# A hybrid decoder step on one core: the attention's heads run together, and two more pairs of convolution blocks move to a seven-product scheme

## The chip, the cores and the metric

The kernel runs on one core of a Trainium2 chip. The core has a matrix engine (TensorE, PE in the profile, with its weight loads shown as PEld), a vector engine (VectorE, DVE), an engine for functions of one operand (ScalarE, ACT), a general one (GpSimd, POOL) and one that mainly issues transfers (SyncE, SP). Each engine works through its own instructions in order; they wait for one another through semaphores. The metric is the time of one launch in microseconds of device time, the median of several runs. Lower is better.

## The reference, cut to what matters

One layer of a decoder for 512 new tokens of a prompt and 8 single tokens of running sequences, 520 rows of width 2048. All is float32.

```python
def mixer(xn, conv_prev, gla_prev, w_in, conv_w, gate_w2, gate_b, gla_norm_g, w_out, chunk):
    proj = xn @ w_in
    bg, cg, hin, q, k, v, og, glr = jnp.split(proj, [_S1, _S2, _S3, _S4, _S5, _S6, _S7], axis=-1)
    cu, conv_new = causal_dwconv(cg * hin, conv_prev, conv_w)
    ya = bg * cu
    logf = jax.nn.log_sigmoid((glr @ gate_w2 + gate_b).astype(f32)) / GATE_TAU
...
    o, s_new = gla_chunked(qh, kh, vh, lf, gla_prev.astype(f32), chunk)
    o = o * lax.rsqrt(var + EPS) * gla_norm_g.astype(f32).reshape(GLA_HEADS, GLA_DV)
    yb = (o.reshape(Bn, L, GLA_V_DIM) * jax.nn.silu(og.astype(f32))).astype(xn.dtype)
    out = jnp.concatenate([ya, yb], axis=-1) @ w_out
```

`w_in` has 6160 columns: three blocks of 1024 for the convolution mixer (bg from column 0, cg from 1024, hin from 2048), q and k (512 each, from 3072 and 3584: 128 for each of four heads), v (1024 from 4096), og (1024 from 5120) and 16 for the gate. After the mixer come a residual sum, a norm, an up projection to 2 x 5632 columns with a convolution and a gate, a down projection, a second residual and a last norm.

## The kernel before

Activations lie transposed, 128 channels to a partition block, 520 tokens along the row, cut into two halves of 260. A float32 product is made of three matmuls of reduced precision: every operand is split into a high part (`hi`, ScalarE) and a rest (`lo`, VectorE), and hi x hi, lo x hi and hi x lo are added up in the matrix engine's banks.

**Classical groups.** `group()` (line 213) makes 128 output columns from all 2048 inputs: 16 steps `k`, each of 3 matmuls for 2 token halves, 96 matmuls of 128 x 128 by 260. Its weights come as two halves of 512 KB. `fetch()` asks SP for the next half named in the list `ahead`, `high()` and `low()` split it, `next_half()` takes one that is split. At the steps `k` in `BEATS` (3, 7, 11, 15) the group calls `beat()` (line 157): one entry of `soon`, one step of the first generator in `queue`, one entry of `side`. At its end it takes one step of the generator in `extra`.

**The attention.** `gla_head()` (line 934) is a generator for one head and needs 22 calls. Steps 1 to 3 make the decay, step 4 the first scores. In steps 7 to 13 it runs through seven levels: in each, matmuls of the products `L` give scores (line 1051 for the first level, 1066 for the others), VectorE merges them into `at` (1073), VectorE makes the `L` that is due two steps later (991) from `e`, and POOL and ScalarE prepare an `e` for a later step (285, 984). Sample states `s0` are loaded with `vb`, their values, read back from memory (1015, 1019), scaled on ScalarE (1025) and updated on VectorE (1028). Step 14 transposes `kc`, steps 15 to 18 treat four chunks of 128 tokens with a running sum `S` (1134, 1139, 1148, 1150, 1152), and steps 19 to 22 normalise the output and store it to `o_d` (1195).

**Order of the first part.** For each head `h` the loop at line 1233 runs groups for k, q and the two halves of v (the first head's k and q come from the start of the kernel), puts `gla_head(h)` in the queue and then runs `conv_tile(h - 1)`; after the loop comes `conv_tile(3)`. `conv_tile(j)` (line 865) is three groups (cg, hin, bg) with the convolution put in `side`, and for an odd `j` the sums and splits that the output projection needs (`mixed_done`). That is 26 groups. From head 1 on `extra` holds `mixer_sums()` (line 774), which reads the normalised input back in four parts and makes the sums that the mixer pairs need; it takes 21 calls. The scratch of the attention (pool `gla`) is given up at the end of this part, and the tiles that come next use the same memory.

**Mixer pairs.** Then two more groups (og of the first head) run while the first pair is prepared. A pair (line 812, `MIX`) makes two blocks of 128 columns at once as a 2 x 2 block product with seven products instead of eight: 7 x 8 x 3 = 168 matmuls by 260. ("ch", j) makes the cg and hin blocks of convolution tile j, ("b", j) the bg blocks of tiles j and j+1, ("og", j) two og blocks. Each product needs its own split weights, prepared two products ahead (`prepare`, lines 1370 and 1374); the seven weight operands are sums of four loaded tiles, made on VectorE (1315), one of them by an accumulating transfer on POOL's queue (1319) for every pair but the first. Generators in `steps` (`mix_gate`, `leave`) finish a pair beside the next one and store its forms to `g_d`. The same scheme then serves the output, up and down projections.

The order of instructions on every engine, POOL and SP included, is the order of the program in both parts (`InOrder`).

Of the kernel before, what the change touches and what calls it, by code (L numbers as in the profile page):

```python
# [17 lines left out]
P = 128  # L18
# [6 lines left out]
NH = 4  # L25
DV = 256
# [11 lines left out]
def trunk_kernel(  # L38
# [53 lines left out]
    def tmp():  # L92
        return tp.tile([P, T], F32, tag="t", name="t")
# [37 lines left out]
    def halves(t):  # L131
        return t[:, :HT], t[:, HT:T]
# [11 lines left out]
    soon, queue, side, extra = deque(), deque(), deque(), deque()  # L144
# [12 lines left out]
    def beat():  # L157

        if soon:
            soon.popleft()()  # L160
        if queue:
            try:
                next(queue[0])
            except StopIteration:
                queue.popleft()
        if side:
            side.popleft()()
# [5 lines left out]
    def new_mm():  # L173

        return [mmp.tile([P, 512], F32, tag="mm", name="mm") for _ in range(2)]

    def span(ps, w, acts, k0, pk0, nk, nkt):

        outs = [x[:, :HT] for x in ps]
        for k in range(k0, k0 + nk):  # L180
            mm3(outs, (w[0][:, k - pk0, :], w[1][:, k - pk0, :]), acts[k], k == 0, k == nkt - 1)

    ahead, coming, highs, halved = deque(), deque(), deque(), deque()
# [13 lines left out]
    def low():  # L197
        if highs:
            raw, nk, hi = highs.popleft()
            lo = wp.tile([P, 1024], F32R, tag="lo", name="lo")  # L200
            nc.vector.tensor_tensor(lo, raw, hi.bitcast(F32), op=ALU.subtract)
            halved.append([x.rearrange("p (k c) -> p k c", k=nk) for x in (hi, lo)])
            fetch()

    def next_half():

        w = halved.popleft()
        high()
        return w

    BEATS = (3, 7, 11, 15)

    def group():
        ps = new_mm()
        for k in range(KD):
            if k % 8 == 0:
                w = next_half()
            span(ps, w, xa, k, k // 8 * 8, 1, KD)
            if k in BEATS:
                beat()  # L220
            if k % 8 == 3:
                low()
        if extra and next(extra[0], extra) is extra:
            extra.popleft()
        return ps


# [98 lines left out]
    with ExitStack() as es:  # L326
# [3 lines left out]
        def tps():  # L330
            return tpp.tile([P, 1024], F32, tag="tp", name="tp")
# [43 lines left out]
        cols = (3584, 3072)  # L375
# [44 lines left out]
        ps = tps()  # L420
# [175 lines left out]
    def evac(ps, out, r=R):  # L596
        for o, p, rr in zip(halves(out), ps, halves(r)):
            nc.vector.tensor_tensor(o, p[:, :HT], rr, op=ALU.mult)
# [18 lines left out]
    def conv(z, w, taps, j, st):  # L617


        c = tmp()  # L620
        conv_tap(c, z, w, taps, j)
        conv_rest(c, z, w, taps, j, st)
        return c
# [34 lines left out]
    def next_z():  # L658
        zcount[0] += 1
        return zpad[zcount[0] % 2]  # L660
# [113 lines left out]
    def mixer_sums():  # L774
# [35 lines left out]


    MIX = (
        ("ch", 4), ("og", 2), ("ch", 5), ("og", 4), ("b", 4), ("og", 6), ("ch", 6), ("ch", 7),
        ("b", 6),
    )

    def mix_source(n, m, k):
# [23 lines left out]
    with ExitStack() as mix:  # L841
# [23 lines left out]
        def conv_tile(j):  # L865
            ps = group()
            cgr = tmp()
            evac(ps, cgr[:, :T])
            ps = group()
            hr = tmp()  # L870
            evac(ps, hr[:, :T])
            z = next_z()
            nc.vector.tensor_tensor(z[:, 2:], cgr[:, :T], hr[:, :T], op=ALU.mult)
            keep_last(z, j, 8, new_conv_p, new_conv_s)
            c = []
            side.append(lambda: c.append(conv(z, cw, 8, j, stc[:, j, :])))
            ps = group()
            bgr, ya = tmp(), tmp()[:, :T]
            if j % 2 == 0:
                even[j] = ya = z[:, 2:]  # L880
            evac(ps, bgr[:, :T])
            nc.vector.tensor_tensor(ya, bgr[:, :T], c[0][:, :T], op=ALU.mult)
            mixed_done(j, ya)

        in_order = InOrder(nc.gpsimd.engine, nc.sync.engine).after_all()
        with ExitStack() as gl:
# [12 lines left out]
                    base=-32 * j, pattern=[[-1, NS]], channel_multiplier=1,  # L899
                )  # L900
            w2s = gp.tile([96, 512], F32R, name="w2s")
            for h in range(NH):
                tile_cols = (3584 + h * P, 3072 + h * P, 4096 + h * DV, 4096 + h * DV + P)
                for c0 in (*tile_cols, *(x + (h - 1) * P for x in (1024, 2048, 0)))[
                    slice(3, 4) if h == 0 else slice(None)
                ]:
                    ahead += [(0, c0), (8, c0)]
            ahead += [(k0, c0) for c0 in (1408, 2432, 384, 5120, 5248) for k0 in (0, 8)]
            halved += v0
            for _ in range(3):  # L910
                fetch()
# [300 lines left out]
            def first_scaled(k, q):  # L1212
                nc.vector.tensor_tensor(k, kq[0], R, op=ALU.mult)
                nc.vector.scalar_tensor_tensor(
                    q, kq[1], QSCALE, R, op0=ALU.mult, op1=ALU.mult
                )
# [16 lines left out]
            for h in range(NH):  # L1233
                if h == 1:
                    extra.append(mixer_sums())
                ps = group() if h else None
                k = gp.tile([P, T], F32, tag="qk", name="k", bufs=5)
                if h:
                    evac(ps, k)
                ps = group() if h else None  # L1240
                assert done[0] >= h - 1
                q = gp.tile([P, T], F32, tag="qk", name="q", bufs=5)
                if h:
                    for o, p, rr in zip(halves(q), ps, halves(R)):
                        nc.vector.scalar_tensor_tensor(
                            o, p[:, :HT], QSCALE, rr, op0=ALU.mult, op1=ALU.mult
                        )
                else:
                    soon += [
                        lambda: None, factors_out, lambda: first_scaled(k, q), first_gate,  # L1250
                        gate_weights,
                    ]
                vt = gp.tile([P, 4, DV], F32, tag="vt", name="vt", bufs=2)
                v = []
                for d in range(2):
                    ps = group()
                    t = gp.tile([P, T], F32, tag="v", name="v", bufs=2)
                    evac(ps, t)
                    v.append(t)
                    soon.append(lambda: None)  # L1260
                    soon.append(lambda t=t, vt=vt, d=d: v_rows(t, vt, d, 0, 4))
                soon.append(lambda v=v, h=h: v_samples(v, h))
                queue.append(gla_head(h, q, k, vt))
                if h:
                    conv_tile(h - 1)
            conv_tile(NH - 1)
            for _ in range(3):
                side.popleft()()
            assert not queue and not extra and not soon, (len(queue), len(extra), len(soon))
# [527 lines left out]
    ps = new_mm()  # L1797
# [19 lines left out]
    ps = new_mm()  # L1817
# [37 lines left out]
    for i, (kind, at, r) in enumerate(order):  # L1855
        j, n = i % 7, i // 7
# [41 lines left out]
        if i in (0, 2, NW, NW + 2):  # L1898

            x = xq[1, 0][0]  # L1900
# [204 lines left out]
```

## Time and profile before

| | us |
|---|---|
| median of 3 runs | 2143.29 |
| lowest and highest | 2142.72, 2144.54 |
| the profiled execution, its own time | 2143.29 |
| its span, first to last instruction | 2141.5 |
| mean granted TensorE clock | 0.998 of full |

The page gives, for one execution, the busy time of each engine, a picture of the span in 40 slices of 53.5 us, the transfer queues, the chain of work that ended last followed back from the end, and the costliest groups of instructions. A row of the timeline or of the chain begins with the start in us and the length in us; a row of a group ends with busy time, mean length of one instruction in ns, and the idle time of the engine ahead of it. L991 is line 991 of the kernel before. The spans of the parts that matter here: the classical groups from about 52 us to 437.5 us, nine mixer pairs to about 622 us, the output projection to about 785 us, the up projection after it.

### The profile page before, as it was taken

The page shows a single profiled execution, that of the slowest core. Times are in us where ns is not written, and L with a number is a line of the kernel's source. Part 1 is how long each engine was busy: PE and PEld are TensorE (multiplying, and loading weights), DVE is VectorE, ACT ScalarE, POOL GpSimd, SP SyncE. Part 2 cuts the span into 40 slices and gives each one's busy share as a digit, 9 for nine tenths or more (in the row PEclk, how much of TensorE's full clock was granted, in tenths as well). Part 3 has the DMA queues.
Part 4 walks back from the last instruction along what each step waited for, and adds up shares of the span by engine and source line. Part 5 has one row for each costly group of instructions (what it writes and reads, how often), then busy time and mean ns, then how long its engine had stood idle before and what let it go on. Part 6 is the DMA issues. An engine that isn't in the chain of part 4 may idle for free.

```text
span 2141.5 us, 44283 instructions
## 1 busy us (share of the span) xinstructions
PE 2117.8 (99%) x17952; PEld 2097.2 (98%) x17952; DVE 1747.0 (82%) x2333; ACT 1105.2 (52%) x1662; POOL 434.9 (20%) x622
## 2 busy tenths in 40 slices
PE   9999999999999989999999999999999999999997
PEld 8999999999999989999999999999999999999997
DVE  6457576688979898998998988988989778888886
ACT  7434434355544686555555555555555554444445
POOL 4213223111334311111211221212212300200000
PEclk9999999999999999999999999999999999999999
DMA  8445473597898996676676676676676966994734
GB/s 257 129 134 176 132 206 114 147 253 187 223 287 239 267 287 164 173 190 177 179 185 174 181 184 174 180 187 175 178 188 180 298 203 163 276 291 133 225 109 159
DMA packets 467325, 415.74 MB, mean 194 GB/s; under 512 B 21721, under 2 KB 426473, under 8 KB 466977
## 3 DMA queue, kind: packets, MB, share of 16 engines
q1 hardware_dynamic: 424209, 289.84, 47.7%
q0 software_dynamic: 42864, 123.00, 21.9%
q8 instruction: 141, 2.31, 0.4%
q14 instruction: 63, 0.52, 0.1%
q10 hardware_dynamic: 48, 0.07, 0.0%
HBM read 299.65 MB, written 80.31 MB: 177 GB/s over the span
## 4 chain that ended last, share of the span: by engine, by line
PE 87%; DMA 5%; DVE 4%; issue 2%; POOL 1%; ACT 1%; SPq 1%; ACTq 0%; DVEq 0%; POOLq 0%
PE mm L1394 34%; PE mm L140 15%; PE ms L1394 14%; PE x L1637 7%; PE y L1637 7%; PE f L1637 3%; PE e L1637 3%; DVE lo L1374 1%; DMA x_d<-acc 1%; DMA form<-g_d 1%; DMA raw<-in_w_in_dram 1%; DMA wgraw<-in_w_in_dram 1%; DVE acc L1656 1%; PE ms L1066 1%; DMA g_d<-fh 0%
## 5 line engine op out<-in xcount | busy, mean ns | idle before, releaser
L1394 PE MATMUL mm<-yl,hi 128*128 128x260 f32 x1696 | 477.2, 281 | 3.5 <-DVE yl L124 3.5
L1394 PE MATMUL mm<-yh,hi 128*128 128x260 f32 x1696 | 475.9, 281 | 1.3 <-ACT ms L1404 0.7
L1394 PE MATMUL mm<-yh,lo 128*128 128x260 f32 x1696 | 475.3, 280 | 1.4 <-DVE lo L1374 1.4
L1370 ACT ACTIVATE hi<-raw 128x1024 fp32r<-128x1024 f32 x324 | 341.8, 1055 | 242.2 <-issue 90.1
L1374 DVE TENSOR_TENSOR lo<-raw,hi 128x1024 fp32r<-128x1024 f32 x324 | 396.1, 1222 | 44.3 <-ACT hi L1370 40.8
L1374 DVE TENSOR_TENSOR lo<-s,hi 128x1024 fp32r<-128x1024 f32 x243 | 298.5, 1228 | 124.4 <-ACT hi L1370 124.2
L1370 ACT ACTIVATE hi<-s 128x1024 fp32r<-128x1024 f32 x243 | 256.7, 1056 | 220.6 <-PE ms L1394 93.6
L1394 PEld LDWEIGHTS mm<-yl,hi 128*128 128x128 f32 x1696 | 318.9, 188 | 4.1 <-DVE yl L124 4.1
L1394 PEld LDWEIGHTS mm<-yh,lo 128*128 128x128 f32 x1696 | 319.9, 189 | 1.8 <-DVE lo L1374 1.8
L1394 PEld LDWEIGHTS mm<-yh,hi 128*128 128x128 f32 x1696 | 319.8, 189 | 1.7 <-ACT ms L1404 0.9
L1394 PE MATMUL ms<-b,hi 128*128 128x260 f32 x1408 | 265.7, 281 | 0.0
L1394 PEld LDWEIGHTS ms<-b,hi 128*128 128x128 f32 x1408 | 222.8, 189 | 0.0
L1637 PE MATMUL x<-form,hi 128*128 128x260 f32 x1120 | 211.8, 281 | 0.9 <-ACT f L1662 0.5
L1637 PE MATMUL y<-form,hi 128*128 128x260 f32 x1120 | 211.5, 281 | 0.0
L1315 DVE TENSOR_TENSOR s<-s,raw 128x1024 f32<-128x1024 f32 x162 | 198.0, 1222 | 2.8
L1394 PE MATMUL ms<-b,lo 128*128 128x260 f32 x704 | 197.4, 280 | 0.0
L1637 PEld LDWEIGHTS x<-form,hi 128*128 128x128 f32 x1120 | 176.5, 188 | 1.7 <-issue 0.8
L1637 PEld LDWEIGHTS y<-form,hi 128*128 128x128 f32 x1120 | 176.5, 188 | 0.3
L1637 PE MATMUL x<-form,lo 128*128 128x260 f32 x560 | 157.0, 280 | 0.4 <-DVE lo L1374 0.4
L1637 PE MATMUL y<-form,lo 128*128 128x260 f32 x560 | 156.8, 280 | 0.0
L1394 PEld LDWEIGHTS ms<-b,lo 128*128 128x128 f32 x704 | 132.4, 188 | 0.0
L1394 PE MATMUL mm<-bh,hi 128*128 128x260 f32 x424 | 118.8, 280 | 1.0 <-DVE acc L1656 1.0
(402 smaller groups left out, 5005.1 us busy)
## 6 DMA issues: line engine op xcount, KB each, us to landing
raw<-in_w_up_dram SPq DMA_DIRECT2D x176, 512.0 KB, 5.1
raw<-in_w_down_dram SPq DMA_DIRECT2D x96, 512.0 KB, 5.6
raw<-in_w_in_dram SPq DMA_DIRECT2D x92, 512.0 KB, 4.3
form<-f_d SPq DMA_DIRECT2D x126, 260.0 KB, 6.1
raw<-raw POOLq DMA_DIRECT2D x56, 512.0 KB, 5.9
f_d<-t POOLq DMA_DIRECT2D x80, 260.0 KB, 5.5
raw<-in_w_out_dram SPq DMA_DIRECT2D x32, 512.0 KB, 9.3
form<-g_d POOLq DMA_DIRECT2D x42, 260.0 KB, 7.6
```

Of the source, the lines that this page charges most:

```text
L140: nc.tensor.matmul(o, w, xx, start=first and i == 0, stop=last and i == 2)
L1066: nc.tensor.matmul(pb[t, c * 32 : (c + 1) * 32], L[:, c, t], second(L[:, c : c + 1, t])[:, 0], start=True, stop=True, tile_position=(0, t. ...
L1315: return lambda: nc.vector.tensor_tensor(out, x, y, op=ALU.add)
L1370: nc.scalar.activation(his[i], src, AF.Copy)
L1374: nc.vector.tensor_tensor(los[i], src, his[i].bitcast(F32), op=ALU.subtract)
L1394: nc.tensor.matmul(st["bank"][b], w[:, k, :], x, start=b not in st["used"] and k == 0 and j == 0, stop=k == 7 and j == 2, skip_group_check ...
L1637: nc.tensor.matmul(ps[:, m, :], w[:, k, m * P : (m + 1) * P], x, start=b not in st["used"] and k == 0 and j == 0, stop=k == 3 and j == 2, ...
L1656: nc.vector.tensor_tensor(a, a, inner(bk[b]), op=op)
```

## The change

Convolution tiles 2 and 3 leave the classical part and become three mixer pairs, ("ch", 2), ("ch", 3) and ("b", 2), among the first in `MIX`, which now has 12 entries. The heads' groups run one after another, k, q, v, v of each, and `conv_tile(0)` and `conv_tile(1)` follow after all of them. The first part has 20 groups. `BEATS` has five entries for a group in place of four. In the k and q groups of heads 1 to 3, `group(True)` takes a step of `extra` after `k` = 7 as well as at the end. The list of weight halves follows the new order.

```diff
-    BEATS = (3, 7, 11, 15)
-
-    def group():
+    BEATS = (2, 5, 8, 11, 14)
+
+    def further():
+        if extra and next(extra[0], extra) is extra:
+            extra.popleft()
+
+    def group(twice=False):
...
-        if extra and next(extra[0], extra) is extra:
-            extra.popleft()
+            if k == 7 and twice:
+                further()
+        further()
         return ps
...
     MIX = (
-        ("ch", 4), ("og", 2), ("ch", 5), ("og", 4), ("b", 4), ("og", 6), ("ch", 6), ("ch", 7),
-        ("b", 6),
+        ("ch", 2), ("og", 2), ("ch", 3), ("og", 4), ("b", 2), ("ch", 4), ("og", 6), ("ch", 5),
+        ("b", 4), ("ch", 6), ("ch", 7), ("b", 6),
     )
...
-            for h in range(NH):
-                tile_cols = (3584 + h * P, 3072 + h * P, 4096 + h * DV, 4096 + h * DV + P)
-                for c0 in (*tile_cols, *(x + (h - 1) * P for x in (1024, 2048, 0)))[
-                    slice(3, 4) if h == 0 else slice(None)
-                ]:
-                    ahead += [(0, c0), (8, c0)]
-            ahead += [(k0, c0) for c0 in (1408, 2432, 384, 5120, 5248) for k0 in (0, 8)]
+            cols = [4096 + P]
+            for h in range(1, NH):
+                cols += [3584 + h * P, 3072 + h * P, 4096 + h * DV, 4096 + h * DV + P]
+            for j in range(2):
+                cols += [1024 + j * P, 2048 + j * P, j * P]
+            ahead += [(k0, c0) for c0 in (*cols, 5120, 5248) for k0 in (0, 8)]
...
-                ps = group() if h else None
+                ps = group(True) if h else None
                 k = gp.tile([P, T], F32, tag="qk", name="k", bufs=5)
                 if h:
                     evac(ps, k)
-                ps = group() if h else None
+                ps = group(True) if h else None
...
                 queue.append(gla_head(h, q, k, vt))
-                if h:
-                    conv_tile(h - 1)
-            conv_tile(NH - 1)
+            for j in range(2):
+                conv_tile(j)
```

## The prediction

> **What bounds the kernel now.** I read the page from the top: the busy times, the slices, the chain that ended last, then TensorE's waits.
>
> ```profile
> span 2141.5 us, 44283 instructions
> ...
> PE 2117.8 (99%) x17952; PEld 2097.2 (98%) x17952; DVE 1747.0 (82%) x2333; ACT 1105.2 (52%) x1662; POOL 434.9 (20%) x622
> ...
> PEclk9999999999999999999999999999999999999999
> ...
> PE 87%; DMA 5%; DVE 4%; issue 2%; POOL 1%; ACT 1%; SPq 1%; ACTq 0%; DVEq 0%; POOLq 0%
> ```
>
> ```profile
> PE mm L1394 <- DVE yl L124: 3.5, 3, 1.9
> PE mm L1394 <- DVE lo L1374: 1.4, 2, 1.0
> ...
> PE ms L1134 <- DVE at L1073: 0.2, 1, 0.2
> ```
>
> TensorE (PE) is busy 99% at full clock, the chain is 87% TensorE, and its longest waits are a few microseconds in all. So time goes down only with fewer matmuls, and up only where another engine makes TensorE wait. The rows below are stretches of time: length, then busy time (and instructions) of PE, PEld, DVE, ACT, POOL, then clock, DMA share, GB/s.
>
> ```profile
> 437.50:462.00 24.50, 21.66 (x174) 20.66 (x173) 24.38 (x35) 14.75 (x24) 2.01 (x3) 1.00 0.86 247
> 462.00:622.00 160.00, 160.00 (x1348) 160.00 (x1347) 141.85 (x183) 84.25 (x124) 43.37 (x64) 1.00 0.82 217
> ...
> 482.00:582.00 100.00, 100.00 (x843) 100.00 (x842) 1.00 0.80 205
> ```
>
> The mixer pairs after the first (462 to 622) run without a gap, with VectorE (DVE) busy 141.85 of 160 us, 89%. The first pair takes 24.5 us.
>
> **The matmuls saved.** The end of a classical group is seen where VectorE takes its banks; two such ends with no attention work between them:
>
> ```profile
> 414.66 0.77 DVE L598 TENSOR_TENSOR t<-mm,R 128x260 f32<-128x260 f32 x2 [1.06 <-PE mm L140]
> ...
> 426.12 0.77 DVE L598 TENSOR_TENSOR zpad<-mm,R 128x260 f32<-128x260 f32 x2 [3.27 <-PE mm L140]
> ```
>
> One group, 96 matmuls, takes 426.12 - 414.66 = 11.46 us. conv_tile(2) and conv_tile(3) are six groups: 6 x 11.46 = 68.8 us go. Three pairs come, each 7 products of 24 matmuls, 168. From the 100 us row a matmul takes 100/843 = 0.1186 us (the count holds those that the edges cut, so slightly more): 3 x 168 x 0.1186 = 59.8 us; at the group's own 11.46/96 it is 60.2. The gain is 8.6 to 9.0 us; I take **8.8**.
>
> **What the new pairs add elsewhere.** They are of kinds that exist (two "ch", one "b"), 141.85/8 = 17.7 us of VectorE each beside 20 us of matmuls, so TensorE hides them. The heavy neighbours "b" and "og" now have a "ch" between them, and "ch", "b" at once after one another stands at the end of the list already. Twelve half loads of 512 KB on SP's queue go with the six groups and twelve come with the pairs; three accumulating DMAs of 512 KB (line 1319) are added on POOL's queue, in a place where every pair but the first has one. I cost this at 0. Without the cover it would be at most the first pair's excess, 24.5 - 19.9 = 4.6 us for each, 14 us; no row of 462 to 622 shows any of it. The wo chunks behind the pairs read the forms in g_d as before.
>
> **The attention steps, moved closer.** The generators of the four heads need 22 steps each, 88, one per beat. Before, 24 groups after the first two give 96 beats; now 18 give 90. Their own matmuls stay; only the distance shrinks.
>
> ```profile
> 352.73 3.07 PE mm L140 x24
> 355.80 0.61 PE ms L1066 x16
> ...
> 104.05 0.42 DVE L991 TENSOR_TENSOR L<-e,k 128x256 f32<-128x256 f32 x1
> ...
> 109.60 0.66 PE L1066 MATMUL ms<-L 128*64 128x32 f32 x16
> ```
>
> A level step is 24 matmuls and 0.6 us of its own, 3.07 + 0.61 = 3.68 us. Between beats in one group there will be 18 matmuls, 2.14 us, and 24 across a group's end: (4 x 18 + 24)/5 x 0.119 + 0.65 = 2.93 us on average. A step's product L is used two steps later. In head 0 the L that is ready at 104.47 is read at 109.60: 5.1 us spare. Two steps are shorter by 2 x 0.73 = 1.5, so about 3.6 us remain in heads 0 to 2, if VectorE is no later than now. The weights have more: a half that is split in one half group is used in the next but one.
>
> ```profile
> 100.00:130.00 30.00, 30.00 (x313) 28.47 (x312) 19.72 (x40) 14.61 (x28) 9.70 (x10) 1.00 0.51 142
> ...
> 350.00:380.00 30.00, 30.00 (x315) 28.32 (x314) 24.39 (x45) 12.55 (x21) 10.67 (x14) 1.00 0.48 144
> ```
>
> At 3.68 us a step, VectorE needs 19.72/30 x 3.68 = 2.4 us per step where a head runs beside the projections (heads 0 to 2 afterwards) and 24.39/30 x 3.68 = 2.99 where it runs beside a convolution (head 3, now beside conv_tile(0) and (1)). Against 2.93 the first keeps up and the second doesn't. In the second stretch the spare is gone already:
>
> ```profile
> 371.44 0.99 DVE L991 TENSOR_TENSOR L<-e,q 128x256 f32<-128x256 f32 x1
> 372.36 1.91 DVE L991 TENSOR_TENSOR L<-e,k 128x256 f32<-128x256 f32 x1
> ...
> 372.68 1.30 POOL L285 TENSOR_TENSOR kc<-kc,k 128x512 f32<-128x512 f32 x1
> ...
> 374.53 0.66 PE L1066 MATMUL ms<-L 128*64 128x32 f32 x16
> ```
>
> L ends at 374.27, 0.26 us ahead of its matmul. After the change head 3's levels begin in conv_tile(0)'s last group and end in conv_tile(1)'s first, so the three splits that end mixer_sums (2.1 us of VectorE), the banks of the last group (0.77) and its gate (0.7) fall among them. Laying VectorE's instructions of these beats end to end, with L at 1.0 and a lo at 1.2, the last two L come 0.5 and 0.8 us late: **1.3 us** of waiting, bounds 0 (the levels as in head 0) and 5 (six late steps at the 0.8 of the last).
>
> The second place is the head's running sum S. Its first chunk waits behind the last sample pair, and that for a DMA:
>
> ```profile
> 116.92 0.66 PE L1066 MATMUL ms<-L 128*64 128x32 f32 x16
> ...
> 120.74 0.49 SPq L1019 DMA_DIRECT2D vb<-v_d  x1
> ...
> 126.29 0.91 ACT L1025 ACTIVATE vb<-vb,k 128x256 f32<-128x256 f32 x2
> ...
> 126.83 0.88 DVE L1028 SCALAR_TENSOR_TENSOR s<-s,asm,vb 128x256 f32<-128x256 f32 x2 [2.82 <-ACT vb L1025]
> ...
> 129.50 0.42 DVE L1150 COPY S<-ms 128x256 f32<-128x256 f32 x1 [1.79 <-PE ms L1148]
> ...
> 132.39 0.39 PE L1139 MATMUL ms<-qb,S 128*128 128x128 f32 x2
> ```
>
> From the level at 116.92 the vb DMA is used after 9.4 us and the pair's s done after 10.8; the matmul that needs S comes after 15.5. The DMA's landing doesn't shrink with the beats, the four distances do, by 0.71 for each in one group: 12.7 to 13.4 us. Queued behind the vb wait are ScalarE's next hi and, on VectorE, s, one lo (1.22) and the copy to S (0.42): 10.8 + 1.6 = 12.4. So it fits by a few tenths in heads 0 to 2 and misses by about 0.5 in head 3, where s is late: **1.1 us** in all, bounds 0 and 4 (1 us for each head).
>
> The third place is the start of the pairs, which hangs on head 3's last store:
>
> ```profile
> 412.76 4.67 DMA o_d<-o
> 417.64 0.37 SPq L828
> ...
> 421.17 12.97 DMA raw<-in_w_in_dram
> 434.24 1.07 ACT hi L1370
> ```
>
> SP's loads for the first pair wait for o_d's store, since they reuse the attention's memory; any delay of it comes back one for one. Head 3's 22nd step is beat 88 of 90, at k=8 of the last group, before beat 94 of 96 at k=7; its convolution then precedes the normalisation instead of splitting it, so the store is issued some 9.5 us into the group, not 10.4. I take 0, bounds -1 and +3.
>
> mixer_sums gets 24 openings, as before; in the k and q groups two, each with 1.4 us of VectorE or two ScalarE scalings of a tile, covered by the 3.6 us above. Its loads on SP's queue may now be asked for half a group later: 0, bounds 0 and 1.
>
> **Sum**, from the profiled execution's 2143.29 us (span 2141.5 and 1.8 around it; also the median): 2143.3 - 8.8 + 1.3 + 1.1 = **2136.8 us**.
>
> **The rivals.**
>
> *Half given back.* Waits at the seam and at S near their upper bounds, 5 + 2: 2143.3 - 8.8 + 7 = 2141.5 us, between 2139.0 and 2147.6. For: the spare of 0.26 us, and 2.99 against 2.93. Against: in head 0 VectorE is idle a third of the time.
>
> *VectorE sets the pace of every head (slower).* It decides when VectorE needs more than about 3.5 us per step: 11 steps of a head carry VectorE work, 3.6 us of spare are eaten first, and 8.8/4 = 2.2 us per head use up the gain, (3.6 + 2.2)/11 = 0.53 above 2.93. What would bring it there is the pair in the rows above: L took 1.91 us, not 0.42, while POOL's kc ran from 372.68 to 373.98, and ended just after it. That step lost 0.57 + 1.49 = 2.06 us. If half the steps lost 2.06, on top of 2.99, it is 4.0 us a step: (4.0 - 2.93) x 11 - 3.6 = 8.2 us a head, 33 us in all, 2143.3 - 8.8 + 33 = 2167 us. Against: the mean over all heads, 0.16 us above the 0.42 of an L that meets nothing.
>
> ```profile
> L991 DVE TENSOR_TENSOR L<-e,k 128x256 f32<-128x256 f32 x28 | 16.3, 584 | 0.0
> ```
>
> [...]
>
> *More than counted (faster).* If o_d's store really comes earlier and the first pair's 4.6 us shrink by a few, with no new waits: 2143.3 - 8.8 - 3 = 2131.5 us, 2130 to 2133.5. Against: the raw DMA's 12.97 us is shared with others that don't move.
>
> That the change does something else can be left out: the loops fix the counts, 26 groups to 20 and 9 pairs to 12.
>
> **How the numbers follow.** About 0.2% (4.3 us) can be told from no change. Forecast, waits of -1 to +4.5 us, 2133.5 to 2139.0: 0.63. Half given back: 0.18. Slower: 0.11. More than counted: 0.08. Faster by over 0.2% (under 2139.0): 0.63 + 0.08 = 0.71; within: 0.18; slower: 0.11. The range 2132 to 2145 leaves out the slower rival, the upper quarter of the second and half of the last, 0.2.
>
> **What would show it.** Right: pairs still 20 us with VectorE near 89%; 12 x 168 pair matmuls; TensorE waits for L (L1066), for at (L1134) or S (L1139) of 1 to 4 us, nearly all in head 3; level steps 2.8 us apart; the first pair still near 24.5. Wrong: waits of over 1 us in heads 0 to 2, L above 0.8 us on average, a first pair over 27 us, or gaps in the added pairs.

## The result and the profile after

The changed kernel takes **2139.38 us** (median of 10 runs, 2135.45 to 2142.20); the kernel before, run beside it, 2144.35 us (10 runs, 2141.95 to 2147.03). The ratio is 0.9978, 95% interval 0.9969 to 0.9987: 2.8 to 6.6 us faster. The profiled execution took 2138.38 us. The page of the changed kernel begins:

```profile
span 2136.7 us, 44234 instructions
...
PE 2109.9 (99%) x17880; PEld 2088.1 (98%) x17880; DVE 1763.6 (83%) x2349; ACT 1121.8 (53%) x1688; POOL 436.0 (20%) x623
```

The two traces cut at the first matmul of each part, in us:

| part | before | after | difference |
|---|---|---|---|
| start and classical groups | 437.50 | 376.36 | -61.1 |
| mixer pairs (9, then 12) | 184.61 | 243.02 | +58.4 |
| output projection | 164.78 | 164.24 | -0.5 |
| up projection | 887.79 | 885.94 | -1.9 |
| down projection to the end | 466.83 | 467.11 | +0.3 |

The six groups removed are worth 68.8 us, but the first part became only 61.1 us shorter. The pairs grew by 58.4 us, where three times 19.99 is 60.0. The up projection is the same in both kernels; over the 14 profiled executions of this study it takes 885.6 to 887.8 us. The execution of the kernel before lost 1.7 us of clock there (granted 0.50 from 800.5 to 803.9 us), that of the changed kernel none. So a difference of 2 us between two single executions may have nothing to do with the change.

Where 7.7 us of the first part went is seen in two views. TensorE's waits of the changed kernel (what waited, for what: us in total, times, longest):

```profile
PE ms L1070 <- DVE L L995: 3.1, 4, 1.6
...
PE ms L1143 <- DVE S L1154: 2.1, 1, 2.1
...
PE ms L635 <- POOL t L290: 0.8, 1, 0.8
```

The waits for L, S and t (the sum of squares of head 2's output) are new: 3.1 + 2.1 + 0.8 = 6.0 us. The same shows in the stretches of time (length, busy time and instructions of PE, PEld, DVE, ACT, POOL, then the granted clock, DMA share, GB/s), first of the kernel before, then of the changed one:

```profile
51.90:437.50 385.60, 385.35 (x3484) 373.03 (x3483) 232.49 (x404) 162.18 (x271) 92.87 (x119) 1.00 0.53 152
```

```profile
51.20:376.30 325.10, 318.83 (x2908) 305.09 (x2907) 201.64 (x360) 151.41 (x258) 86.13 (x111) 0.99 0.54 158
376.40:401.50 25.10, 23.54 (x192) 22.74 (x191) 24.95 (x35) 14.07 (x23) 2.68 (x4) 1.00 0.80 215
401.50:619.00 217.50, 217.50 (x1830) 217.50 (x1830) 189.02 (x243) 112.74 (x164) 50.46 (x74) 1.00 0.77 203
...
122.00:124.00 2.00, 0.35 (x4) 0.15 (x2) 1.97 (x4) 1.48 (x3) 0.00 (x0) 1.00 0.14 50
124.00:126.00 2.00, 1.57 (x8) 1.09 (x8) 2.00 (x5) 0.38 (x1) 0.00 (x0) 0.80 0.60 150
126.00:128.00 2.00, 2.00 (x13) 1.02 (x12) 1.93 (x3) 0.38 (x1) 0.00 (x0) 0.50 0.67 202
128.00:130.00 2.00, 2.00 (x16) 2.00 (x16) 0.04 (x1) 0.00 (x0) 0.00 (x0) 0.84 0.33 57
```

In the classical groups TensorE was idle for 385.60 - 385.35 = 0.25 us before and for 325.10 - 318.83 = 6.27 us after. The last rows show a second price: after the wait of 122 to 124.4 us the granted clock falls to 0.50 and is back at 130. The clock missing is 2 x (0.20 + 0.50 + 0.16) = **1.7 us** of TensorE's work. -68.8 + 6.0 + 1.7 = -61.1. (The stretch itself shrank by 385.60 - 325.10 = 60.5 us; the start ahead of it, which is the same work, was 0.7 us shorter, so 0.6 us has no name.) The added pairs, in the row from 401.50, run without a gap.

Where each wait comes from is seen in the timeline of the changed kernel. Head 0 first:

```profile
107.28 0.69 DVE L704 TENSOR_TENSOR yx<-yx 128x520 f32<-128x520 f32 x1
107.48 1.62 POOL L290 TENSOR_TENSOR qb<-qb,q 128x512 f32<-128x512 f32 x1
108.00 1.67 DVE L698 SCALAR_TENSOR_TENSOR yx<-yx 128x520 f32<-128x520 f32 x1
...
114.75 0.88 DVE L1032 SCALAR_TENSOR_TENSOR s<-s,asm,vb 128x256 f32<-128x256 f32 x2
...
116.60 0.50 SPq L1023 DMA_DIRECT2D vb<-v_d  x1
...
121.36 0.91 ACT L1029 ACTIVATE vb<-vb,k 128x256 f32<-128x256 f32 x2 [4.49 <-DMA vb<-v_d]
121.90 0.88 DVE L1032 SCALAR_TENSOR_TENSOR s<-s,asm,vb 128x256 f32<-128x256 f32 x2 [5.32 <-ACT vb L1029]
122.70 1.22 DVE L201 TENSOR_TENSOR lo<-raw,hi 128x1024 fp32r<-128x1024 f32 x1
123.95 0.42 DVE L1154 COPY S<-ms 128x256 f32<-128x256 f32 x1
124.43 0.49 PE L1143 MATMUL ms<-qb,S 128*128 128x128 f32 x2 [2.08 <-DVE S L1154]
```

Lines 704 and 698 are one step of `mixer_sums`. The same two instructions take 0.69 us each at 124.29; here the second takes 1.67, beside POOL's product in the row above it, so the step costs 2.4 us of VectorE. It stands ahead of q's banks and of the third sample pair's s at 114.75, though the vb of that pair was ready. That pair's store and the load of the last vb come after it in SP's order, so vb is issued at 116.60 and lands about 4.2 us after its issue is done. VectorE then sits idle for 5.32 us in front of an s that waits for vb, with the copy of S queued behind that s. TensorE gets S at 124.43.

The other place is the seam between conv_tile(0) and conv_tile(1), in head 3:

```profile
309.66 0.64 ACT L123 ACTIVATE yh<-yx 128x520 fp32r<-128x520 f32 x1 [1.10 <-DMA mt_d<-yx]
310.33 0.70 DVE L124 TENSOR_TENSOR yl<-yx,yh 128x520 fp32r<-128x520 f32 x1 [0.66 <-ACT yh L123]
311.06 0.77 DVE L603 TENSOR_TENSOR t<-mm,R 128x260 f32<-128x260 f32 x2
311.86 0.70 DVE L887 TENSOR_TENSOR zpad<-t 128x520 f32<-128x520 f32 x1
...
313.46 0.42 DVE L995 TENSOR_TENSOR L<-e,k 128x256 f32<-128x256 f32 x1
...
317.70 1.45 POOL L290 TENSOR_TENSOR kc<-kc,k 128x512 f32<-128x512 f32 x1
317.95 1.49 DVE L995 TENSOR_TENSOR L<-e,k 128x256 f32<-128x256 f32 x1
```

The last split of `mixer_sums` waits through ScalarE for a transfer of `mixer_sums` itself (0.66 us of idle VectorE), and the banks, the gate and L stand behind it: TensorE waits 1.6 us for the L at 313.46 and 1.1 us for the one at 317.95, which is stretched to 1.49 us beside POOL's product.

### The profile page after: what moved, and what is told of

The parts are those of the page before. It is cut to its first block, busy times and chain, and to the rows that moved or that the text cites. A ratio compares the mean times of both kernels' runs of the same rounds, so it can differ in the third digit from the quotient of the medians.

```text
span 2136.7 us, 44234 instructions
## 1 busy us (share of the span) xinstructions
PE 2109.9 (99%) x17880; PEld 2088.1 (98%) x17880; DVE 1763.6 (83%) x2349; ACT 1121.8 (53%) x1688; POOL 436.0 (20%) x623
## 4 chain that ended last, share of the span: by engine, by line
PE 62%; DMA 1%; DVE 1%; issue 1%; ACT 0%; POOL 0%; ACTq 0%; DVEq 0%; SPq 0%; POOLq 0%
PE mm L1397 29%; PE ms L1397 12%; PE x L1640 7%; PE y L1640 7%; PE f L1640 3%; PE e L1640 3%; PE mm L140 2%; DMA ssq<-fh 1%; DMA x_d<-acc 0%; PE ms L1998 0%; DMA yl<-t_d 0%; DVE yl L124 0%; DVE lo L1377 0%; DVE s L1318 0%; ACT y L2061 0%
## 5 line engine op out<-in xcount | busy, mean ns | idle before, releaser
L1397 PE MATMUL mm<-yl,hi 128*128 128x260 f32 x1792 | 504.1, 281 | 2.8 <-DVE yl L124 2.8
L1397 PE MATMUL mm<-yh,hi 128*128 128x260 f32 x1792 | 502.5, 280 | 0.6 <-DVE t L701 0.6
L1397 PE MATMUL mm<-yh,lo 128*128 128x260 f32 x1792 | 502.0, 280 | 0.8 <-DVE lo L1377 0.8
L1373 ACT ACTIVATE hi<-raw 128x1024 fp32r<-128x1024 f32 x336 | 354.4, 1055 | 245.4 <-issue 89.3
L1377 DVE TENSOR_TENSOR lo<-raw,hi 128x1024 fp32r<-128x1024 f32 x336 | 410.2, 1221 | 44.6 <-ACT hi L1373 40.8
L1377 DVE TENSOR_TENSOR lo<-s,hi 128x1024 fp32r<-128x1024 f32 x252 | 309.4, 1228 | 131.3 <-ACT hi L1373 129.9
L1373 ACT ACTIVATE hi<-s 128x1024 fp32r<-128x1024 f32 x252 | 266.3, 1057 | 233.2 <-PE ms L1397 97.3
L1397 PEld LDWEIGHTS mm<-yl,hi 128*128 128x128 f32 x1792 | 336.6, 188 | 3.7 <-DVE yl L124 3.7
L1397 PEld LDWEIGHTS mm<-yh,lo 128*128 128x128 f32 x1792 | 337.8, 189 | 1.2 <-DVE lo L1377 1.2
L1397 PEld LDWEIGHTS mm<-yh,hi 128*128 128x128 f32 x1792 | 337.7, 188 | 0.8 <-issue 0.8
```

Of the source, the lines that this page charges most:

```text
L1373: nc.scalar.activation(his[i], src, AF.Copy)
L1377: nc.vector.tensor_tensor(los[i], src, his[i].bitcast(F32), op=ALU.subtract)
L1397: nc.tensor.matmul(st["bank"][b], w[:, k, :], x, start=b not in st["used"] and k == 0 and j == 0, stop=k == 7 and j == 2, skip_group_check ...
```

## The experiments

All times are medians; each ratio is to the kernel before on the same chip, with its 95% interval. "First pair" is the time from the first matmul of the first mixer pair to that of the second; all other pairs are 19.99 us in every kernel.

| kernel | us | ratio | TensorE idle in the classical groups | first pair |
|---|---|---|---|---|
| before | 2144.35 | 1 | 0.25 | 24.61 |
| changed | 2139.38 | 0.9978 [0.9969, 0.9987] | 6.27 | 23.05 |
| order_alone | 2144.80 | 1.0007 [0.9998, 1.0016] | 5.70 | 20.44 |
| five_beats | 2150.54 | 1.0031 [1.0019, 1.0042] | 7.89 | 20.44 |
| five_late | 2143.07 | 0.9999 [0.9990, 1.0008] | 2.37 | 20.44 |
| sums_early | 2132.92 | 0.9948 [0.9936, 0.9961] | 2.11 | 22.40 |
| load_first | 2137.77 | 0.9971 [0.9961, 0.9981] | 5.11 | 22.62 |
| pair_late | 2135.68 | 0.9965 [0.9952, 0.9977] | 3.27 | 22.79 |
| sums_load | 2132.09 | 0.9949 [0.9936, 0.9961] | 1.89 | 22.50 |
| sums_load_late | 2130.95 | 0.9942 [0.9930, 0.9955] | 0.79 | 22.64 |
| six_beats | 2139.26 | 0.9978 [0.9970, 0.9987] | 7.81 | 20.44 |
| products_on_vector | 2136.72 | 0.9970 [0.9960, 0.9981] | 3.65 | 22.64 |
| six_at_end | 2132.03 | 0.9947 [0.9933, 0.9960] | 0.78 | 23.80 |
| six_at_end_sum | 2131.47 | 0.9940 [0.9927, 0.9952] | 0.16 | 24.34 |

### The order without the pairs: order_alone

The changed kernel with four classical convolution tiles and the nine pairs of before, so only the order of the heads, the five beats and the doubled steps differ from before.

```diff
-        ("ch", 2), ("og", 2), ("ch", 3), ("og", 4), ("b", 2), ("ch", 4), ("og", 6), ("ch", 5),
-        ("b", 4), ("ch", 6), ("ch", 7), ("b", 6),
+        ("ch", 4), ("og", 2), ("ch", 5), ("og", 4), ("b", 4), ("og", 6), ("ch", 6), ("ch", 7),
+        ("b", 6),
...
-            for j in range(2):
+            for j in range(4):
```

> Heads first, five beats, doubled sums as in the changed kernel, but all four convolution tiles classical and nine pairs as before, so no matmul is saved. If the pairs are worth 8.8 us as counted and the new order loses what the changed kernel lost: 4 to 6 us slower than before, about 1.002. If the pairs are worth less (the loss is in them): about 1.000.

Measured 2144.80 us, ratio 1.0007. The time alone would speak for the second reading, that the pairs are worth less; the trace doesn't. Its waits on TensorE are nearly those of the changed kernel:

```profile
PE ms L1070 <- DVE L L995: 3.1, 3, 1.7
PE ms L1143 <- DVE S L1154: 1.5, 1, 1.5
```

So the new order makes the waits, and not the pairs. They cost 5.70 - 0.25 = 5.5 us, but the first pair is 24.61 - 20.44 = 4.2 us shorter, since the heads end two convolution tiles earlier: 1.3 us slower in sum, as measured (-0.4 to +3.4). The matmuls' term agrees with it: between this kernel and the changed one there are six groups and three pairs, and the two differ by 5.4 us in the medians, where 8.8 less the 2.6 us that the first pair gets longer gives 6.2 (3.9, if the profiled execution's 0.6 us more of idle time and its dip of the clock, 1.7, are taken off as well).

### The beats alone: five_beats

```diff
-    BEATS = (3, 7, 11, 15)
+    BEATS = (2, 5, 8, 11, 14)
```

The kernel before with this edit only.

> The kernel before with five beats to a group and nothing else, so no step of mixer_sums is doubled and the order is the old one. Theory A: TensorE's waits in the first part stay under 2 us, time 0.999 to 1.001 of before. Theory B: waits for L and S of 5 us or more, time 1.002 or above.

Measured 2150.54 us: slower by 6.6 us in the ratio, as theory B has it. Heads 1 to 3 of the kernel before run beside convolution tiles, and each of them waits for S:

```profile
PE ms L1139 <- DVE S L1150: 6.1, 3, 2.6
```

Head 0 doesn't wait, neither for S nor for L. It runs beside the k, q and v groups of head 1 here as in the changed kernel, with the same five beats; what differs is that no step of `mixer_sums` is doubled, and none of its VectorE work falls into this stretch:

```profile
113.41 0.88 DVE L1028 SCALAR_TENSOR_TENSOR s<-s,asm,vb 128x256 f32<-128x256 f32 x2
...
122.45 0.42 DVE L1150 COPY S<-ms 128x256 f32<-128x256 f32 x1
...
123.16 0.39 PE L1139 MATMUL ms<-qb,S 128*128 128x128 f32 x2
```

The third pair's s comes 3.1 us after the matmuls of the sixth level at 110.27 (5.8 us after those at 108.99 in the changed kernel), and S is ready 0.3 us before TensorE asks for it. So beside the projections five beats alone fit, by a few tenths, and the doubled step takes them past it; in heads 1 to 3 of the old order, beside a convolution tile, they don't fit.

Its profile also shows the longest dip of the clock in this study, behind one of these waits:

```profile
283.00:286.00 3.00, 0.44 (x4) 0.25 (x3) 2.41 (x5) 2.12 (x4) 0.00 (x0) 0.93 0.20 71
286.00:289.00 3.00, 2.92 (x16) 1.98 (x16) 2.93 (x7) 0.38 (x1) 0.00 (x0) 0.50 0.73 190
289.00:292.00 3.00, 3.00 (x19) 2.48 (x12) 2.75 (x6) 0.38 (x1) 0.00 (x0) 0.50 0.03 7
```

### mixer_sums from head 0 on: sums_early

```diff
-                if h == 1:
+                if h == 0:
                     extra.append(mixer_sums())
```

It starts in the groups of head 0 instead of head 1, so that its steps are over before head 3 and fall elsewhere in head 0.

> The changed kernel with one edit: mixer_sums begins with head 0's two v groups, two steps earlier everywhere, so its sums leave the end of head 1's q group and its last splits the seam between the two convolution tiles. Theory A (the lost microseconds come from where mixer_sums' steps fall on VectorE): TensorE's wait for S (2.1 us in the changed kernel) and for L (3.1 us) go to under 1 us together, the first part is 4 to 5 us shorter, time about 0.996 of before. Theory B (beats 18 matmuls apart are too close whatever else VectorE has): the waits stay at 5 us or more in all, time about 0.998 as now.

Measured 2132.92 us, ratio 0.9948, 6.5 us below the changed kernel. No wait for L is left, and that for S is shorter:

```profile
PE ms L1143 <- DVE S L1154: 1.3, 1, 1.3
```

One number of the program takes away both late L and a good third of the wait for S. The steps of `mixer_sums`, not the convolution's banks and gate, were what VectorE had too much of at the seam.

For S the edit shows less (under 1 us together was expected). Counted from the matmuls of head 0's sixth level at 110.00 (108.99 in the changed kernel), the third pair's s comes 3.2 us earlier, but vb can be used only 1.1 us earlier: 6.5 us after its issue at 114.84, where it was 4.8. Four loads of `mixer_sums` itself now stand ahead of it on SP's queue, from 108.87 on; that they are what holds it up isn't shown.

### The last load earlier, and both: load_first, sums_load

The last load of a head's states and vb goes on SP's queue ahead of the third pair's update and store.

```diff
                     if i == 5:
                         pos = bank()
                         sample_out(0)
+                        loaded.append(sample_load(6))
                     if i in (2, 3, 5):
                         s0.append(sample_pair({2: 0, 3: 2, 5: 4}[i], *loaded.popleft()))
-                    if i in (0, 2, 5):
-                        loaded.append(sample_load({0: 2, 2: 4, 5: 6}[i]))
+                    if i in (0, 2):
+                        loaded.append(sample_load({0: 2, 2: 4}[i]))
```

> The changed kernel with the last sample load issued ahead of the store of the pair before it, so SP no longer waits for VectorE's s there. If head 0's wait for S comes from that chain (late s, then store, then load, then landing): the wait for S goes from 2.1 us to under 0.5, L's 3.1 us stay, time 0.997 of before. If S waits for VectorE's queue itself: no change, 0.998.

Measured 2137.77 us, ratio 0.9971 beside 0.9978: the intervals overlap, so no gain is shown. In the trace the wait for S is 1.0 us in place of 2.1 (under 0.5 was expected), the waits for L stay at 3.0.

> mixer_sums from head 0 on, and the last load of a head's states issued ahead of the third pair's steps, both at once. Theory A: the S wait of 1.3 us that mixer_sums from head 0 on left is the load of vb alone, and the earlier issue takes 1 us of it off: S wait under 0.5, classical part's end 370.0 to 370.7, time 2131 to 2132.5. Theory B (it is VectorE's lateness): the S wait stays 1.0 to 1.3, end 371, time 2133.

Measured 2132.09 us. The wait for S is 1.1 us, hardly less than the 1.3 with `mixer_sums` early alone. Theory A fails: the load was no earlier at its end (ScalarE took vb at 121.31, as against 121.30 without the edit).

### The copy of S ahead of the last s: pair_late, sums_load_late, five_late

If the copy of S is late because it is queued behind an s that waits for a transfer, then changing places is enough, and no load has to be faster.

```diff
                 nc.scalar.activation(kt, pb.rearrange("p (c k) -> p c k", c=4), AF.Copy)
-                s0.append(sample_pair(6, *loaded.popleft()))
                 yield
...
+                    if c == 0:
+                        s0.append(sample_pair(6, *loaded.popleft()))
                     if c == 1:
                         sample_out(4)
```

> The changed kernel with one step moved: the last sample pair of a head (its ACT vb, its VectorE s, its store) is issued after the first chunk's copy of S and not before it. Theory A: TensorE's wait for S in head 0 (2.1 us) exists because the copy of S stands behind the s of the last sample pair in VectorE's order, and that s waits for the load of vb (6.7 us of idle VectorE or less before it); so the S wait falls from 2.1 to under 0.3, the four states' products are waited for at most 1 us in its place, the L waits stay 3.1, the classical part ends 1 to 2 us before 376.36, and the time is 2136 to 2138. Theory B: VectorE is late as a whole at this place, by the doubled steps of mixer_sums and the denser beats; then the S wait stays above 1.5 and the time at 2139.

Measured 2135.68 us, ratio 0.9965, whose interval overlaps that of the changed kernel. No wait for S is left. The waits for L are 2.5 us. The trace has a dip of the clock all the same, behind the wait for L at the seam (TensorE idle from about 310.0 to 312.0):

```profile
312.00:314.00 2.00, 2.00 (x24) 0.89 (x24) 2.00 (x3) 1.42 (x3) 1.92 (x3) 0.65 0.03 8
314.00:316.00 2.00, 2.00 (x9) 1.56 (x8) 1.91 (x5) 0.00 (x0) 2.00 (x2) 0.50 0.45 141
```

> The kernel before with five beats a group (which alone gave S waits of 6.1 us in heads 1 to 3 and a time of 2150.5) and the last sample pair's step after the copy of S. Theory A: in heads 1 to 3 too, the copy of S stood behind an s that waited for vb (VectorE idle 2.68 us before the s of head 1); the S waits fall from 6.1 to under 0.6, the classical part ends 4 to 6 us before 450.17, time 2145 to 2147. Theory B: the dense beats beside a convolution tile make VectorE late as a whole: S waits stay above 4, time 2149 to 2151.

Measured 2143.07 us, ratio 0.9999: the edit takes back all of the 6.6 us that five beats had cost in the old order. The wait for S falls from 6.1 to 0.9 us, all of it in head 3. In the head whose S wait came ahead of that long dip the rows of VectorE are now

```profile
278.72 0.42 DVE L1149 COPY S<-ms 128x256 f32<-128x256 f32 x1
282.69 0.88 DVE L1028 SCALAR_TENSOR_TENSOR s<-s,asm,vb 128x256 f32<-128x256 f32 x2 [3.54 <-ACT vb L1025]
```

VectorE still idles 3.54 us for vb, but nobody waits for it: S was made 4 us earlier. This is theory A in both kernels: VectorE was not too busy here, it stood in the wrong order.

> mixer_sums from head 0 on, the earlier load, and the last sample pair's step after the copy of S, all three. Theory A: no L wait and no S wait are left on TensorE (S under 0.2), classical part's end 369.5 to 370.2, first of the three pairs 22.2 to 22.6 us, time 2130.5 to 2132. Theory B: an S wait of about 1 us stays, time 2133; or the products with the states wait instead (over 1 us at line 1040 or so), and nothing is won.

All three edits: 2130.95 us, ratio 0.9942, the lowest median of the study and 8.4 us below the changed kernel. TensorE's idle time in the classical groups is nearly that of before, and the clock is whole:

```profile
51.30:368.30 317.00, 316.21 (x2907) 304.02 (x2907) 202.48 (x360) 151.91 (x258) 86.53 (x111) 1.00 0.56 162
```

### A sixth beat, and the first pair: six_beats, six_at_end, six_at_end_sum

`six_beats` is sums_load_late with one more beat in every group.

```diff
-    BEATS = (2, 5, 8, 11, 14)
+    BEATS = (1, 4, 7, 9, 12, 14)
```

> The kernel with mixer_sums from head 0 on, the earlier load and the later sample step (2130.95 us), with six beats a group in place of five. A head gets 24 beats for its 22 steps, so head 3's store of o_d comes about one group earlier. Theory A: the first pair's excess over 19.99 us (2.65 there) hangs on that store and falls to 0.4 to 0.6, as in the two kernels whose heads end early; VectorE needs 2.4 us a step beside projections against 2.56 a step, so heads 0 to 2 stay without L waits over 0.5 us, and head 3, beside the convolution tiles, waits 1 to 4 us for L: time 2129 to 2132. Theory B (the rival in which VectorE sets the pace of every head): L waits in heads 1 and 2 too, over 1 us a head, 8 us or more in all, time over 2136. Theory C: the excess isn't o_d's, and stays above 2.

Measured 2139.26 us. The first pair fell to 20.44 us, as theory A said, but the classical groups became 327.20 - 317.00 = 10.2 us longer: 7.0 us of idle TensorE, and 3.2 us more of busy time, 1.7 of them a dip of the clock.

```profile
PE ms L1070 <- DVE L L995: 4.9, 2, 2.8
...
PE ms L1127 <- POOL kc L290: 1.8, 1, 1.8
```

So neither theory fits: the two waits for L stand in heads 0 and 3 and not in every head, but they are long enough to cost more than the first pair gives. `six_at_end` keeps five beats everywhere but in the last two groups of conv_tile(1), where only head 3's last steps are left; `six_at_end_sum` has a head's sum of squares on VectorE as well.

```diff
-            ps = group()
+            ps = group(beats=(1, 4, 7, 9, 12, 14) if j == 1 else BEATS)
```

```diff
-                ptt(sq, sq, sq2, ALU.add)
+                nc.vector.tensor_tensor(sq, sq, sq2, op=ALU.add)
```

> The kernel with mixer_sums from head 0 on, the earlier load and the later sample step (2130.95 us; first pair 22.64 us), with six beats instead of five in the last two groups of conv_tile(1) alone, where only the last eight steps of head 3 are left. Theory A (the first pair's excess over 19.99 us is the time by which head 3's store of o_d is late): the store comes 2.5 to 3.5 us earlier ahead of the pairs than its 26.4 us, the excess falls from 2.65 to 0.4 to 0.6, no new wait: time 2128 to 2129.5. Theory B: the raw transfers themselves set it, and the excess stays above 2, time 2131.

> The same, and the sum of squares of a head's output (128 x 520, 1.28 us on POOL) on VectorE instead. Theory A: TensorE's wait of 0.8 us for POOL's t in head 2 goes (VectorE takes about 0.7 us for it), the L and S waits stay at none: 0.5 to 0.8 us below the kernel with six beats at the end. Theory B: VectorE is late there and the wait stays, only by another engine: no change.

Measured 2132.03 and 2131.47 us: no gain on 2130.95. The first pair became longer (23.80, 24.34), not shorter. In the second the wait of 0.8 us for POOL's t is gone, as expected. What goes with the first pair's length is seen when the issue of head 3's store of o_d is held against the first matmul of the pairs. The rows of the changed kernel, of the one before, and of six_at_end and six_beats:

```profile
349.96 1.21 POOL L1199 DMA_DIRECT2D o_d<-o  x2 [7.00 <-DVE o L1195]
```

```profile
412.09 1.21 POOL L1195 DMA_DIRECT2D o_d<-o  x2 [8.00 <-DVE o L1191]
```

```profile
343.29 1.21 POOL L1201 DMA_DIRECT2D o_d<-o  x2 [6.11 <-DVE o L1197]
```

```profile
331.01 1.21 POOL L1201 DMA_DIRECT2D o_d<-o  x2 [6.87 <-DVE o L1197]
```

| kernel | store issued ahead of the pairs by | first pair over 19.99 |
|---|---|---|
| before | 437.50 - 412.09 = 25.4 | 4.62 |
| six_at_end_sum | 25.8 | 4.35 |
| six_at_end | 369.31 - 343.29 = 26.0 | 3.81 |
| changed | 376.36 - 349.96 = 26.4 | 3.06 |
| pair_late, products_on_vector, sums_load_late, load_first, sums_load, sums_early | 26.4 | 2.80, 2.65, 2.65, 2.63, 2.51, 2.41 |
| five_beats, five_late | 39.7 | 0.45 |
| six_beats | 378.91 - 331.01 = 47.9 | 0.45 |
| order_alone | 95.2 | 0.45 |

The later the store, the longer the first pair, with 0.6 us of scatter between kernels of one lead; 39.7 us are enough. What the pair sees is the landing: SP issues its first load for the pair 0.2 to 0.3 us after the store has landed, in the kernel before (417.43, then 417.64), the changed one (353.22, then 353.50) and six_at_end (348.12, then 348.40). From issue to landing of the whole store it takes 5.3, 3.3 and 4.8 us. The sixth beat at the end didn't bring the store forward but put it 0.4 us back, and the runs don't show why. All rows agree with what theory A of six_at_end says of the excess; but its lever had no effect, and no run moved the store alone.

### The products on VectorE: products_on_vector

```diff
-                        ptt(qb, qb, q4, ALU.mult)
+                        nc.vector.tensor_tensor(qb, qb, q4, op=ALU.mult)
...
-                        ptt(kc, kc, k4, ALU.mult)
+                        nc.vector.tensor_tensor(kc, kc, k4, op=ALU.mult)
```

> The changed kernel with a head's two products qb x q and kc x k (128 x 512, 1.29 to 2.17 us on POOL) on VectorE. Theory A: the L of 1.3 to 1.5 us (in place of 0.42) are those that run beside these two, since VectorE and POOL hold each other up there; the k and q products fall to at most 0.9 us, the mean of L from 577 and 469 ns to under 460 both, VectorE gets 8 instructions of 0.7 us more, and the L waits fall from 3.1 to about 2: time within 2 us of the changed kernel's 2139.4. Theory B: the stretched L have another cause (the L beside e's differences on POOL stay): means stay above 520 and 450, and the L waits grow by the 0.7 us a product, to 4 or more.

Measured 2136.72 us, ratio 0.9970 [0.9960, 0.9981] beside 0.9978 for the changed kernel: no loss, a gain not shown. The same L of head 3's seam in its timeline:

```profile
315.54 0.42 DVE L995 TENSOR_TENSOR L<-e,k 128x256 f32<-128x256 f32 x1
...
317.74 0.69 DVE L1118 TENSOR_TENSOR qb<-qb,q 128x512 f32<-128x512 f32 x1
```

L takes 0.42 us in place of 1.49, and the product takes VectorE 0.69 us where it took POOL up to 2.17. The mean of the k half of L falls from 469 to 431 ns, of the q half from 577 to 501 (under 460 was expected; beside e's differences, which stay on POOL, seven L of the changed kernel take 0.63 to 0.87 us). The waits for L fall from 3.1 to 1.9 us, the second late L at the seam is gone, and head 0's wait for S too; in its place TensorE waits 0.7 us for VectorE's kc once. So theory A holds for this L: POOL's product beside it cost it 1.49 - 0.42 = 1.07 us. Head 0's step of `mixer_sums`, too, takes 1.4 us here and not 2.4.

## Why the prediction was right, and where it was not

**The direction and the matmuls were right.** 2136.8 us were forecast and 2139.38 measured, a gain of 5.0 us where 6.5 was said. The time lies in the stated range, but 0.4 us above the stretch of the likeliest case (2133.5 to 2139.0), in that of "Half given back". That it is so near is in part luck: waits and clock took 5.3 us more than the sum had, and the first pair, costed at 0, gave 1.6 back. Three more pairs at 19.99 us and six fewer groups at 11.46 are the 8.8 us of the sum. The added pairs cost nothing elsewhere: pairs 2 to 12 run without a gap. Their heavy neighbours, the twelve half loads and the three accumulating transfers are hidden.

**The waits were mis-sized: 2.4 us forecast, 6.0 plus 1.7 of clock measured.** The step that failed is the last and smallest one, "mixer_sums gets 24 openings, as before; ... covered by the 3.6 us above", costed at 0. The 3.6 us are the spare of L, and L in heads 0 to 2 kept it. What had no spare was the chain that makes S, which the prediction itself had found to fit "by a few tenths": 2.4 us of `mixer_sums` ahead of it in head 0 and it misses by 2.1. So the wait came in head 0, where the prediction saw none to speak of, and not in head 3; its size of 1.1 us for all heads was half the measured one, and a wait of over 1 us in heads 0 to 2 is on its own list of signs of being wrong. five_beats shows the cause: head 0 without the doubled step has 0.3 us to spare. pair_late shows that the wait goes when the copy of S no longer stands behind the last s. sums_early takes the step away as well, but leaves 1.3 us of the wait, since vb can be used only 6.5 us after its issue there.

**At the seam the place was right, and the size not:** 1.3 us forecast, waits for two late L of 1.6 and 1.1 measured. VectorE's instructions were laid end to end, but the last split of `mixer_sums` isn't free to start: it waits for a transfer, 0.66 us. And the L that was laid at 1.0 us took 1.49 beside POOL.

**The clock was not in the sum at all.** A wait was priced at its length. The wait of 2.1 us in head 0 cost 1.7 us more.

**The start of the pairs was costed at 0** with the store of o_d 0.9 us earlier by the prediction's own working. The store was issued 1.0 us earlier, counted from the pairs' first matmul, and landed 3.1 us earlier (20.1 us ahead of it before, 23.1 after), and the first pair is 1.6 us shorter. So "one for one" holds neither for the issue nor for the landing.

**What is left.** -8.8 + 6.0 + 1.7 - 1.6 + 0.6 without a name is -2.1 us; the two profiled spans differ by 4.8 since the parts that the change doesn't touch were 2.8 us shorter in the one taken after, 1.7 of them by the dip of the clock that the execution before has in the up projection. So each of the two has one dip, in different places. If the dips of both kernels cost the same, the sum is -3.8, which the measured -2.8 to -6.6 holds; -2.1 it doesn't hold. The mean clock of every execution is on record, to three decimals: 0.997 in nine of the changed kernel's ten and 0.996 in one, 0.995 to 0.998 in 61 executions of the kernel before; the profiled ones without a dip show 0.998, those with one 0.997 or 0.998. So dips are common in both kernels, and which has more can't be told. The account of the medians stays open by a microsecond or two.

**The rivals.** "Half given back" has the mechanism: 7.7 us lost, where it said 7. The time came out 2.1 us lower, since the first pair gave 1.6 back and for what is left open above. "VectorE sets the pace of every head" didn't come: L's k half takes 469 ns on average, less than the 584 of before, and no head but 3 has late L of over 0.3 us. Nor did it at six beats, where two heads wait and not all. "More than counted" is what the edits of sums_load_late make of the change: 8.8 us of matmuls and 24.61 - 22.64 = 2.0 of the first pair, with 0.5 us of new waits, are 10.3 us; measured 12.4 (9.6 to 15.0).

## What to carry to other kernels

Where work is put closer together, price first the chain that had the least spare, not the one that is easiest to follow; a step "covered" by the spare of one chain may stand in front of another. Look for instructions that wait for a transfer in an in-order engine and ask what is queued behind them: the copy of S is 0.42 us long and held TensorE up for 2.1 us only because of its place, and changing places took away what an earlier load only halved. And a new wait of TensorE of 2 us is to be priced with the clock: here one of 2.1 us cost 3.8, and five of eleven gaps of 1.9 to 3.1 us went with a dip.

## What was not expected of the hardware

The granted clock fell to 0.50 behind single waits of about 2 to 3 us in a program that keeps TensorE busy otherwise. The matmuls show it in the timeline of the changed kernel:

```profile
121.97 0.38 PE L1138 MATMUL ms<-at,vt 128*128 128x128 f32 x2
...
128.00 0.42 PE L140 MATMUL mm<-ch,lo 128*128 128x260 f32 x1
128.21 0.42 PE L140 MATMUL mm<-bl,hi 128*128 128x260 f32 x1
...
128.88 0.28 PE L140 MATMUL mm<-bh,lo 128*128 128x260 f32 x1
129.00 0.28 PE L140 MATMUL mm<-ch,lo 128*128 128x260 f32 x1
```

At 128.00 the matmuls start 0.21 us apart, at 128.88 again 0.12. Over the classical groups of all profiled kernels there are eleven gaps of 1.9 to 3.1 us between the starts of two matmuls; a dip goes with five of them (gaps of 2.36, 2.92, 2.07, 3.11 and 1.92 us) and begins between 0.5 us ahead of the gap's end and 2.0 us behind it, and none goes with the other six (up to 2.84), nor any gap under 1.8 in these groups. Four of the dips take 1.7 us of clock away, which is 3.4 us at half; the one of five_beats takes 3.4.

The length of one gap doesn't decide alone. At the start of the up projection TensorE waits five times within 15 us (in the kernel before with gaps of 0.98 to 2.20 us between the starts of two matmuls), and four of the 14 profiled executions have a dip there: before, sums_load, sums_load_late and six_at_end. In six_at_end no gap there is longer than 1.3 us, but together TensorE was idle for 13.70 - 10.02 = 3.7 us ahead of it:

```profile
776.00:789.70 13.70, 10.02 (x75) 9.24 (x76) 12.83 (x18) 12.64 (x23) 2.42 (x3) 1.00 1.09 301
789.70:793.20 3.50, 3.50 (x19) 3.50 (x18) 3.50 (x5) 2.50 (x4) 0.00 (x0) 0.51 1.16 279
```

What sets the length of a dip, and which waits bring one, the runs don't show.
